# A two-layer encoder step: a new opening, biases read from one line, a gate computed in 32-column strips

## The chip, the cores and the metric

The kernel runs on one core of one Trainium2 chip. The metric is the device time of one execution, in microseconds (us), as the median of several runs. Five engines work side by side in a core: TensorE (PE in the profile, its weight loads PEld), VectorE (DVE), ScalarE (ACT), GpSimd (POOL) and SyncE (SP). Each runs its own list of instructions in order, and waits on semaphores for the others. Transfers are issued by an engine into its queue and carried by 16 DMA engines.

## The reference

One inference step of an encoder with two layers, on 256 prompt tokens and 32 sample tokens, feature width D = 1024, float32:

```
layer 0:  h = rmsnorm(x);  q,k,v of 16 heads = h @ w_in_ab
          heads 0-7:  chunked attention, softmax(q k/8 + rel_bias[clip(distance)])
          heads 8-15: stick-breaking attention
          x += concat(heads) @ w_out_ab
layer 1:  h = rmsnorm(x);  q,k,v of 16 heads and 16 forget gates = h @ w_in_c
          logf = log_sigmoid(gate + b_f);  c = cumsum(logf)
          softmax(q k/8 + c[query] - c[key]);   x += heads @ w_out_c
each layer then: x += cross_attention(rmsnorm(x), 256 memory tokens)
                 x += swiglu_ffn(rmsnorm(x))
y = rmsnorm(x);  outputs: y, all new k and v, logf, the memory's k and v
```

The sample tokens also attend to cached keys and values. The relative bias depends only on query minus key, clipped to ±128, so for each of the 8 heads one line of 384 numbers holds all that is needed.

## The kernel before, in words

**Layout.** Activations stay transposed: features on the 128 partitions, the 288 tokens along the free dimension. `x[k]`, k = 0..7, are the eight feature blocks, held in four tiles of two blocks each.

**A projection.** The weights come as "units": 128 output columns by 1024 input features, 512 KB, one tile `st` of 128x1024 (four buffers, one SP transfer). ScalarE casts a unit to `hi` (line 141) and VectorE subtracts to get `lo` (line 142); activations are split the same way into `hh` (line 247, ScalarE) and `hl` (line 250, VectorE). For every feature block `mm3` (line 145) multiplies hi by hh, hi by hl and lo by hh, so a projection (`project`, line 151) is 24 matmuls of 288 columns that add up in one PSUM bank, `pj`. Nearly all matmuls are issued in the helper `mm`, line 68.

**The norm.** The gain is multiplied in at the split, and 1/rms of each token later: squares of x (line 202, or line 200 on POOL), their sum over blocks (`ssq`, line 213), a few matmuls with a vector of 1/1024 (`nrm`), eleven small VectorE operations for the reciprocal root (lines 227 to 232), six matmuls that spread it over the partitions (`nr`), and a copy to `rstd` (line 280). Projections do not wait for that; their evacuation does: `evac_q` (line 720) and `evac_kv` (line 725) register a function with `then`, which runs when `rstd` is there and multiplies by it.

**Order of the work.** Python generators in the list `active` are advanced one step by `tick()`, which every projection calls; each `yield` is a place where a piece of attention waits for the next tick, so that a projection's matmuls cover the work of the other engines in between. A framework then orders each engine's instructions and sets the semaphores. `pairs` (line 807) projects q, k, v of two heads at a time, and adds the pair's attention to the list behind it. `memory.steps` puts projections of the memory tokens in between (`kh`, `mk`, `mkT`).

**Layer 0** (`mix_ab`, line 767): pairs 0 to 3 use chunked attention. `rel_lines` (line 735) loads the bias (`line`), extends it on VectorE (line 740), stores it to DRAM (`lined`) and writes it from there 128 times per head, eight transfers, into a DRAM tensor `skew` in which each row is one longer than the line; `rel_prompt` reads each head's tile `bi` back from it as two transfers, and POOL masks two corners. The softmax adds the bias and takes the maximum (line 350, VectorE), ScalarE takes the exponential (line 352), VectorE divides (line 355), and PE transposes the result (`tp`, lines 374 to 376).

**Layer 1** (`mix_c`, line 874): the 16 gate columns are one unit, `w_c[24]`, padded to 128 columns; it and the first q unit are begun for six of eight blocks ahead of the last blocks of x (`begin`). `gate` (line 821) scales the result by `rstd`, adds the bias (line 826), transposes it (`gt`, lines 829 to 831), takes the log-sigmoid in a chain of small VectorE and ScalarE operations (lines 834 to 847), and forms the sums over tokens by matmuls with a triangle (`gc`, `gs`, `gn`). The sums go to DRAM (`cumd`, line 858) and come back spread over the partitions (`ck`, line 896); POOL makes the bias tiles `bc` of them (lines 901 to 904), and the softmax of pair 0 needs those.

**Stores.** Keys and values (line 730), memory keys and values, and the log gates are stored by SP, in the queue that loads the weights. The result y is stored in six pieces (line 976).

Of the kernel before, what the change touches and what calls it, by code (L numbers as in the profile page):

```python
# [15 lines left out]
P = 128  # L16
NT = 288
# [9 lines left out]
def encoder_step(ctx: ExitStack, tc: tile.TileContext, a):  # L27
# [39 lines left out]
    def mm(out, lhsT, rhs, start=True, stop=True):  # L67
        T.matmul(out, lhsT, rhs, start=start, stop=stop, skip_group_check=True)  # L68
# [5 lines left out]
    first = wp.tile([P, 1024], F32, tag="st", bufs=4, name="first")  # L74

    def first_part(c0, c1):
        DMA.dma_start(first[:, c0:c1], a["w_ab"][0][:, c0:c1])

    first_part(0, 256)
    for i in range(4):  # L80
        DMA.dma_start(xh[i], a["xT"][:, 2 * i * NT:2 * (i + 1) * NT])
        if i == 0:
            DMA.dma_start(gain, a["gains"])
            first_part(256, 512)
        if i == 1:
            first_part(512, 1024)
# [5 lines left out]
    make_identity(nc, identb)  # L92

# [23 lines left out]
    for h in range(4):  # L117
        G.memset(odd[32 * h:32 * h + 32, h % 2:h % 2 + 1], 1.0)

# [7 lines left out]
    V.tensor_tensor(fold, by_head[:, :, 0], by_head[:, :, 1], ALU.add)  # L127
    wtab = cst.tile([P, 2], F32, name="wtab")
# [3 lines left out]
    def unit(src, st=None, pieces=1):  # L132

        if st is None:
            st = wp.tile([P, 1024], F32, tag="st", bufs=4, name=name("st"))
            DMA.dma_start(st, src)
        hi = wp.tile([P, 1024], F32R, tag="hi", bufs=5, name=name("hi"))
        lo = wp.tile([P, 1024], F32R, tag="lo", bufs=4, name=name("lo"))
        for c in range(pieces):
            b = slice(c * 1024 // pieces, (c + 1) * 1024 // pieces)  # L140
            S.copy(hi[:, b], st[:, b])  # L141
            V.tensor_tensor(lo[:, b], st[:, b], hi[:, b].bitcast(F32), ALU.subtract)  # L142
        return hi, lo

    def mm3(out, w, blk, h, k, start, stop):
        b = slice(blk * P, blk * P + P)
        mm(out, w[0][:, b], h[0][k], start, False)
        mm(out, w[0][:, b], h[1][k], False, False)
        mm(out, w[1][:, b], h[0][k], False, stop)

    def project(src, h, n=NT, w=None, begun=None):
        if begun:
            w, p = begun
        else:
            w, p = w or unit(src), acc("pj")
        with tc.issue_after(warmed.ins):
            for k in range(BEGIN if begun else 0, KT):
                mm3(p[:, :n], w, k, h, k, k == 0, k == KT - 1)
        tick()
        return p  # L160
# [19 lines left out]

    def start(g):
# [7 lines left out]
    class Norm:  # L189
# [7 lines left out]
        def add(self, xb, second=False, pool=False):  # L197
# [859 lines left out]
```

## Time and profile before

| | |
|---|---|
| median of 3 runs | 971.54 us (970.67 to 971.94) |
| the profiled execution | 974.15 us, its span 972.3 us |
| mean granted TensorE clock | 0.995 |
| instructions | 19122 |
| bytes moved | 163.59 MB |

The profile is of one execution, which took 974.15 us, 2.6 us over the median of the runs; its span, from the first instruction shown to the last, is 1.85 us shorter than its time. In a row of groups stand line, engine, operation, output from inputs, shape and count, then busy us and the mean ns of one, then the idle time in front and what ended it. In the chain of waits each row is one piece of the path that ended last: start, length, and the engine and line, or the transfer, that held it. A matmul's duration in the timeline is its time in the pipeline; what a matmul costs is the distance from its start to the next one's.

### The profile page before, as it was taken

To read this page: it belongs to the slowest core of one execution; us is meant where nothing else is said; L and a number is where in the kernel's file an instruction comes from. 1 tells how busy PE (TensorE), PEld (TensorE's weight loads), DVE (VectorE), ACT (ScalarE), POOL (GpSimd) and SP (SyncE) were. 2 spreads that over 40 slices of the span, in tenths; PEclk is the share of its full clock that TensorE was granted. 3 is DMA by queue.
4 is the path that set the end of the run, shared out by engine and by line. 5 is a ranking of instruction groups with operands and counts; after the bars stand their busy time and mean duration, and the time that the engine had idled before them with its cause. 6 is when DMAs were issued, how large, how long until landed. Compare 5 with 4: busy or idle time off the path is not lost.

```text
span 972.3 us, 19122 instructions
## 1 busy us (share of the span) xinstructions
PE 955.3 (98%) x7495; PEld 923.2 (95%) x7495; DVE 588.6 (61%) x1133; ACT 484.8 (50%) x856; POOL 195.1 (20%) x291
## 2 busy tenths in 40 slices
PE   8999999999999999999999999999999999999997
PEld 7889999998999999999998999999989999999996
DVE  6587555676666555754565666657757655555452
ACT  5456768545554444444444545446546544444331
POOL 3021001310213222411004333213002222222010
PEclk9999999999999999999999999999999999999999
DMA  7775455544254444554555555555434444444431
GB/s 232 247 241 189 137 180 181 183 162 147 103 174 154 173 162 164 191 192 160 173 202 161 179 190 191 169 164 179 150 117 159 159 159 173 163 164 173 165 117 49
DMA packets 59721, 163.59 MB, mean 168 GB/s; under 512 B 8192, under 2 KB 20528, under 8 KB 59632
## 3 DMA queue, kind: packets, MB, share of 16 engines
q1 hardware_dynamic: 59632, 162.38, 49.0%
q8 instruction: 59, 0.97, 0.4%
q14 instruction: 30, 0.25, 0.1%
HBM read 152.20 MB, written 11.72 MB: 169 GB/s over the span
## 4 chain that ended last, share of the span: by engine, by line
PE 91%; DMA 3%; DVE 3%; issue 1%; ACT 1%; SPq 1%; POOL 0%; DVEq 0%; POOLq 0%; ACTq 0%
PE pj L68 51%; PE dn L68 14%; PE op L68 11%; PE mv L68 5%; PE po L68 1%; PE xo L68 1%; PE xs L68 1%; DMA st<-w_ab 1%; PE zb L68 1%; PE sc L68 1%; DVE lo L142 1%; DMA skew<-lined 1%; DMA x<-xT 1%; PE xss L68 1%; PE xt L614 0%
## 5 line engine op out<-in xcount | busy, mean ns | idle before, releaser
L141 ACT CAST hi<-st 128x1024 fp32r<-128x1024 f32 x260 | 272.2, 1049 | 335.7 <-issue 147.3
L68 PE MATMUL pj<-hh,hi 128*128 128x288 f32 (+1 forms) x1352 | 406.3, 301 | 0.0
L68 PE MATMUL pj<-hl,hi 128*128 128x288 f32 (+1 forms) x1352 | 399.9, 296 | 1.7 <-DVE hl L250 1.7
L68 PE MATMUL pj<-hh,lo 128*128 128x288 f32 (+1 forms) x1352 | 400.2, 296 | 0.0
L142 DVE TENSOR_TENSOR lo<-st,hi 128x1024 fp32r<-128x1024 f32 x260 | 322.7, 1242 | 127.4 <-PE dn L68 41.2
L68 PEld LDWEIGHTS pj<-hh,hi 128*128 128x128 f32 x1352 | 257.0, 190 | 5.8 <-issue 4.2
L68 PEld LDWEIGHTS pj<-hl,hi 128*128 128x128 f32 x1352 | 257.1, 190 | 3.3 <-DVE hl L250 3.2
L68 PEld LDWEIGHTS pj<-hh,lo 128*128 128x128 f32 x1352 | 256.9, 190 | 0.0
L68 PE MATMUL dn<-fh,hi 128*128 128x288 f32 x400 | 108.5, 294 | 0.0
L68 PE MATMUL dn<-fh,lo 128*128 128x288 f32 x352 | 103.3, 294 | 0.0
L68 PE MATMUL dn<-fl,hi 128*128 128x288 f32 x304 | 89.5, 294 | 0.0
L68 PE MATMUL op<-ol,hi 128*128 128x288 f32 x256 | 75.8, 297 | 0.0
L68 PE MATMUL op<-oh,hi 128*128 128x288 f32 x256 | 75.5, 297 | 0.0
L68 PE MATMUL op<-oh,lo 128*128 128x288 f32 x256 | 75.2, 294 | 0.0
L68 PEld LDWEIGHTS dn<-fh,hi 128*128 128x128 f32 x400 | 72.3, 188 | 0.0
L68 PEld LDWEIGHTS dn<-fh,lo 128*128 128x128 f32 x352 | 66.2, 188 | 0.0
L213 POOL TENSOR_TENSOR ssq<-ssq,sq 128x288 f32<-128x288 f32 (+1 forms) x37 | 37.7, 1018 | 119.8 <-ACT sq L202 76.8
L68 PEld LDWEIGHTS dn<-fl,hi 128*128 128x128 f32 x304 | 57.1, 188 | 0.0
L695 POOL TENSOR_TENSOR fl<-us,fh 128x288 fp32r<-128x288 f32 x38 | 32.9, 865 | 119.3 <-ACT fh L694 119.3
L690 DVE TENSOR_TENSOR us<-pj,rstd 128x288 f32<-128x288 f32 x44 | 20.1, 457 | 59.9 <-PE pj L68 59.9
L691 POOL TENSOR_TENSOR gs<-gs,sg 128x288 f32<-128x288 f32 x44 | 38.9, 884 | 75.8 <-ACT sg L689 75.8
L68 PEld LDWEIGHTS op<-ol,hi 128*128 128x128 f32 x256 | 48.2, 188 | 0.6 <-issue 0.4
(257 smaller groups left out, 1204.9 us busy)
## 6 DMA issues: line engine op xcount, KB each, us to landing
st<-w_gate SPq DMA_DIRECT2D x44, 512.0 KB, 3.3
st<-w_up SPq DMA_DIRECT2D x44, 512.0 KB, 3.2
st<-w_down SPq DMA_DIRECT2D x44, 512.0 KB, 3.2
st<-w_c SPq DMA_DIRECT2D x25, 512.0 KB, 3.3
st<-w_ab SPq DMA_DIRECT2D x23, 512.0 KB, 4.4
st<-w_xk SPq DMA_DIRECT2D x16, 512.0 KB, 3.4
st<-w_xv SPq DMA_DIRECT2D x16, 512.0 KB, 3.5
st<-w_xq SPq DMA_DIRECT2D x16, 512.0 KB, 3.5
```

The lines of the kernel that those rows point to most:

```text
L68: T.matmul(out, lhsT, rhs, start=start, stop=stop, skip_group_check=True)
L141: S.copy(hi[:, b], st[:, b])
L142: V.tensor_tensor(lo[:, b], st[:, b], hi[:, b].bitcast(F32), ALU.subtract)
L213: eng.tensor_tensor(s[:, :self.n], self.acc[i][:, :self.n], q[:, :self.n], ALU.add)
L690: V.tensor_tensor(us, pu[:, :NT], cur.r, ALU.mult)
L691: G.tensor_tensor(gs, gs, sg, ALU.mult)
L695: G.tensor_tensor(lo, us, hi.bitcast(F32), ALU.subtract)
```

## The change

1. **Opening.** The first q, k and v units are loaded in three parts each, between the four tiles of x, and multiplied side by side, block by block, into three PSUM banks (`side_by_side`). All eight squares go to ScalarE and all seven sums to VectorE. The norm's first step no longer yields.
2. **Biases.** POOL loads the line at the start, extends it, and stores `lined`; the tensor `skew` is gone. Each head's tile is two transfers of 64 overlapping rows out of `lined`, and one tile serves both query tiles. The order of rows that this gives is falling, so q is written in falling order and turned back when the transposed softmax is copied.
3. **Held work.** `held` and `not_before` add orderings without a wait: the splits of the units in pairs 0 to 3 stand behind the norm's chain and an earlier projection in their engine's list, and loads of caches and memory stand behind later weights. The memory's preparation, the attention of pair 0 and that of the first sample groups start one tick later.
4. **Stores.** Keys, values, memory keys and values and log gates are stored by POOL.
5. **Gate.** The gate's weights come as 128x256, are multiplied by the gain on VectorE (`wgg`), and eight float32 matmuls of 32 columns write four strips of 32 partitions in one bank. Three float32 matmuls with `fold4` add the four strips while they transpose. The sums `gc` come one tick later, the attention of pair 0 as well; the units begun early are now the first q and k; one memory step moves from the end to pair 0.
6. **Tail.** y is stored in three pieces.

The diff, cut to its core:

```diff
-    first = wp.tile([P, 1024], F32, tag="st", bufs=4, name="first")
...
-    first_part(0, 256)
...
+    first = [wp.tile([P, 1024], F32, tag="st", bufs=4, name=f"first{i}") for i in range(3)]
+    def first_part(i, c0, c1):
+        DMA.dma_start(first[i][:, c0:c1], a["w_ab"][4 * i][:, c0:c1])
+    PARTS = ((0, 256), (256, 512), (512, 1024))
+    first_part(0, *PARTS[0])
...
             DMA.dma_start(gain, a["gains"])
-            first_part(256, 512)
-        if i == 1:
-            first_part(512, 1024)
+        if i < 3:
+            for u in range(3):
+                if i or u:
+                    first_part(u, *PARTS[i])
...
+    line = cst.tile([8, 384], F32, name="line")
+    lined = dr.tile([8, 384], F32, name="lined")
+    G.dma_start(line[:, 128:384], a["rel"][:, 0:256])
...
+    G.tensor_copy(line[:, 0:128], line[:, 128:129].to_broadcast([8, 128]))
+    G.dma_start(lined, line)
...
+    def unit_tiles():
+        return [wp.tile([P, 1024], F32R, tag=t, bufs=n, name=name(t)) for t, n in (("hi", 5), ("lo", 4))]
+    def split_weights(st, w, c0=0, c1=1024, hold=False):
+        hi, lo = (t[:, c0:c1] for t in w)
...
+    began, behind, loads = [], [], []
...
+    def not_before(ins, other):
+        tc.add_manual_dep(ins.ins, other.name, mybir.DependencyInfo(mybir.DependencyClass.NoSync, mybir.DependencyReason.DATA),
+                          reason="not_before")
+    def held(ins):
+        if hurry[0]:
+            for i in began[-2:-1] + [i for i in behind if i.engine == ins.ins.engine]:
+                not_before(ins, i)
...
+    def unit(src):
...
+        loads.append(DMA.dma_start(st, src).ins)
+        w = unit_tiles()
+        split_weights(st, w, hold=True)
+        return w
...
+    def store(dst, t):
+        G.dma_start(dst, t)
...
-        def add(self, xb, second=False, pool=False):
+        def add(self, xb, eng=None):
             q = tok("sq")
-            if pool:
-                G.tensor_tensor(q[:, :self.n], xb[:, :self.n], xb[:, :self.n], ALU.mult)
...
             self.parts += 1
...
-            else:
-                eng = V if self.parts == KT else G
-            i = int(second or (self.parts == KT and self.hurry))
+            eng = eng or (V if self.parts == KT else G)
...
-            if self.gi != 1:
+            if self.gi > 1:
...
-            S.copy(self.r, p)
-            for f in self.waiting:
-                f()
+            r = S.copy(self.r, p)
+            done = [f() for f in self.waiting]
             self.waiting = None
+            if self.gi == 0:
+                behind.append(self.norm.last.ins)
+                yield 1
+                behind.extend([r.ins, done[-1].ins])
...
+        q0, q1 = (q[:, 160:288], q[:, 32:160]) if falling else (q[:, 0:128], q[:, 128:256])
...
+                S.copy(w[hd][:, 0:384], t[:, 0:384])
...
-    def cache(src):
...
-        DMA.dma_start(t, src)
+        i = DMA.dma_start(t, src)
+        if ahead:
+            not_before(i, loads[-ahead])
...
...
                 st = wp.tile([P, 1024], F32, tag="st", bufs=4, name=name("mem"))
...
+                if self.l == 0:
+                    not_before(i, loads[-1])
...
-                DMA.dma_start(a["mkT"][l, i], t[:, 0:NP])
...
         t = tok("q")
-        cur.then(lambda: V.scalar_tensor_tensor(t, p[:, :NT], 0.125, cur.r, op0=ALU.mult, op1=ALU.mult))
+        out = t[:, ::-1] if falling else t
...
         t = tok("kv")
         def go():
-            V.tensor_tensor(t, p[:, :NT], cur.r, ALU.mult)
-            DMA.dma_start(dst, t)
+            i = V.tensor_tensor(t, p[:, :NT], cur.r, ALU.mult)
+            store(dst, t)
+            return i
...
+    def rel_prompt(h):
...
+        G.memset(t[64:128, 192:256], NEG)
+        for p, n in ((0, 256), (64, 192)):
+            G.dma_start(t[p:p + 64, 0:n], bass.AP(tensor=lined.tensor, offset=lined.offset + 384 * h + p + 1, ap=[[1, 64], [1, n]]))
...
+        G.dma_start(t[:, 0:160], bass.AP(tensor=lined.tensor, offset=lined.offset + 384 * 4 * g + 97, ap=[[384, 4], [1, NS], [1, 160]]))
...
+        def side_by_side():
+            p = [att("pj"), acc("pj"), acc("pj")]
+            with tc.issue_after(warmed.ins):
+                for k in range(KT):
+                    for u in range(3):
+                        i = mm3(p[u][:, :NT], w0[u], k, cur.h, k, k == 0, k == KT - 1)
+                        if k in (0, 5, 7) and u == 2:
+                            began.append(i.ins)
+            tick()
+            return p
...
+            hurry[0] = j < 4
             b = 12 * (j // 4) + j % 4
             kv = 8 * (j // 4) + j % 4
-            qs[j] = evac_q(cur, project(w[b], cur.h, w=w0 if j == 0 else None))
-            if j == 0:
-                proj.line = rel_lines()
-            ks[j] = evac_kv(cur, project(w[b + 4], cur.h), a["kv0"][kv])
...
+            qs[j] = evac_q(cur, next(p), j < 4)
+            ks[j] = evac_kv(cur, next(p), a["kv0"][kv])
+            if j < 4:
...
-                return attend_prompt(*args, [rel_prompt(proj.line, 2 * j + i) for i in range(2)], o[0][j], o[1][j])
...
+        def attend(j):
+            return later(attention(j), j == 0)
...
-                return attend_sample(*args, rel_sample(proj.line, g), oo)
-            return stick_sample(*args, oo)
+                bias = rel_sample(g)
+                yield 1
...
+    def later(g, n):
+        for _ in range(n):
+            yield 1
...
-        zt = tok("gz")[0:H]
...
+        V.tensor_tensor(zt, p[:, :NT], cur.r, ALU.mult)
...
-        T.transpose(t[:, 0:16], zt[:, 0:128], ident[0:H, 0:H])
-        T.transpose(t[:, 16:32], zt[:, 128:256], ident[0:H, 0:H])
-        T.transpose(t[0:NS, 32:48], zt[:, 256:288], ident[0:H, 0:H])
...
+        G.dma_start(a["lf"][0:256].rearrange("(t p) h -> p t h", p=P), lf[:, 0:32].rearrange("p (t h) -> p t h", h=H))
+        G.dma_start(a["lf"][256:288], lf[0:NS, 32:48])
+        yield 1
...
+        wg, wgg = tok("wg"), tok("wgg")
+        DMA.dma_start(wg[:, 0:256], a["w_g"])
+        g = gain[:, KT:2 * KT].unsqueeze(2).to_broadcast([P, KT, 32])
+        V.tensor_tensor(wgg[:, 0:256].rearrange("p (k c) -> p k c", c=32), wg[:, 0:256].rearrange("p (k c) -> p k c", c=32), g, ALU.mult)
         w = a["w_c"]
-        begun = begin([w[24], w[0]], cur.h)
+        begun = begin([w[0], w[8]], cur.h)
         active.append(cur.scale())
-        p = project(w[24], cur.h, begun=begun[0])
+        p = acc("gp")
+        for k in range(KT):
+            mm(p[32 * (k % 4):32 * (k % 4) + 32, :NT], wgg[:, 32 * k:32 * k + 32], x[k], k < 4, k >= 4)
...
+            qs[j] = evac_q(cur, project(w[j], cur.h, begun=begun[0] if j == 0 else None))
+            ks[j] = evac_kv(cur, project(w[8 + j], cur.h, begun=begun[1] if j == 0 else None), a["kv1"][j])
...
+            return later(attend_prompt(qs[j], ks[j], vs[j], vns, j, bias, o[0][j], o[1][j]), j == 0)
...
-        pairs(proj, attend, sample, memory, (3, 1, 1, 1, 1, 1, 1, 5))
+        pairs(proj, attend, sample, memory, (4, 1, 1, 1, 1, 1, 1, 4))
...
+    w0 = [unit_tiles() for _ in first]
...
+        if m in (1, 3, 5):
+            for st, w in zip(first, w0):
+                split_weights(st, w, *PARTS[m // 2])
     for m in range(KT):
-        cur.norm.add(x[m], m >= 4, m < 4)
+        cur.norm.add(x[m], V)
...
-            DMA.dma_start(a["y"][P * t:min(P * t + P, NT), b], out[r, b])
+        DMA.dma_start(a["y"][P * t:min(P * t + P, NT)], out[r])
```

Three places show how the order moves. On TensorE at the start of the program: `pj` is the bank, `hh` and `hl` the split x, `hi` and `lo` the split weights. Before:

```order
L68 MATMUL pj_252<-hh_166,hi_174 128x288
L68 MATMUL pj_252<-hl_167,hi_174 128x288
L68 MATMUL pj_252<-hh_166,lo_175 128x288
L68 MATMUL pj_252<-hh_170,hi_174 128x288
L68 MATMUL pj_252<-hl_171,hi_174 128x288
L68 MATMUL pj_252<-hh_170,lo_175 128x288
```

And after the change:

```order
L68 MATMUL pj_283<-hh_187,hi_181 128x288
L68 MATMUL pj_283<-hl_188,hi_181 128x288
L68 MATMUL pj_283<-hh_187,lo_182 128x288
L68 MATMUL pj_284<-hh_187,hi_183 128x288
L68 MATMUL pj_284<-hl_188,hi_183 128x288
L68 MATMUL pj_284<-hh_187,lo_184 128x288
L68 MATMUL pj_285<-hh_187,hi_185 128x288
L68 MATMUL pj_285<-hl_188,hi_185 128x288
L68 MATMUL pj_285<-hh_187,lo_186 128x288
L68 MATMUL pj_283<-hh_191,hi_181 128x288
```

Three matmuls per feature block became nine, in three banks.

On VectorE in the norm of the opening: `ssq` are the sums of squares, `lo` a unit's split, `ms` the first of the small operations. Before, four units are split ahead of it:

```order
L142 TENSOR_TENSOR lo_295<-st_292,hi_294 128x1024
L124 TENSOR_SCALAR ident<-warm 128x128
L213 TENSOR_TENSOR ssq_226<-sq_222,sq_224 128x288
L127 TENSOR_TENSOR fold<-ident 128x64
L142 TENSOR_TENSOR lo_348<-st_345,hi_347 128x1024
L213 TENSOR_TENSOR ssq_230<-ssq_226,sq_228 128x288
L142 TENSOR_TENSOR lo_401<-st_398,hi_400 128x1024
L213 TENSOR_TENSOR ssq_234<-ssq_230,sq_232 128x288
L142 TENSOR_TENSOR lo_465<-st_462,hi_464 128x1024
L227 TENSOR_SCALAR ms_330<-nrm_323 128x6
```

After, seven sums and one split:

```order
L243 TENSOR_TENSOR ssq_241<-sq_237,sq_239 128x288
L243 TENSOR_TENSOR ssq_245<-ssq_241,sq_243 128x288
L243 TENSOR_TENSOR ssq_249<-ssq_245,sq_247 128x288
L243 TENSOR_TENSOR ssq_253<-ssq_249,sq_251 128x288
L243 TENSOR_TENSOR ssq_257<-ssq_253,sq_255 128x288
L243 TENSOR_TENSOR ssq_261<-ssq_257,sq_259 128x288
L243 TENSOR_TENSOR ssq_265<-ssq_261,sq_263 128x288
L151 TENSOR_TENSOR lo_390<-st_387,hi_389 128x1024
L257 TENSOR_SCALAR ms_362<-nrm_358 128x6
```

The next units' splits now stand behind the small operations.

In SP's queue at the gate of layer 1: `cumd` and `cumsd` are the stores of the sums, `ck` the load that the bias tiles need, `mkT` a store of memory keys, `st` a unit. Before:

```order
L858 DMA cumd<-gr_6299 16x256
L865 DMA cumsd<-gw_6306 16x160
L553 DMA mkT<-mk_6316 128x256
L136 DMA st_6805<-w_c 128x1024
L553 DMA mkT<-mk_6354 128x256
L553 DMA mkT<-mk_6392 128x256
L896 DMA ck_6399<-cumd 128x512
```

After:

```order
L916 DMA cumd<-gr_6346 16x256
L923 DMA cumsd<-gw_6353 16x160
L962 DMA ck_6408<-cumd 128x512
L173 DMA st_6874<-w_xk 128x1024
L173 DMA st_6943<-w_c 128x1024
```

The load of `ck` now follows the two stores directly; the `mkT` stores are in POOL's queue.

## What will it do to the time?

> **What bounds the kernel now.** The first view is the page: the engines' busy time, and the chain of waits summed by engine.
>
> ```profile
> PE 955.3 (98%) x7495; PEld 923.2 (95%) x7495; DVE 588.6 (61%) x1133; ACT 484.8 (50%) x856; POOL 195.1 (20%) x291
> PE 91%; DMA 3%; DVE 3%; issue 1%; ACT 1%; SPq 1%; POOL 0%; DVEq 0%; POOLq 0%; ACTq 0%
> ```
>
> TensorE holds 91% of the chain, so a change gains only by fewer matmuls, or where the other 9% (some 88 us) really stops TensorE. The second view is the chain of waits over the first 40 us.
>
> ```profile
> 3.63 5.58 DMA x<-xT
> ...
> 16.27 6.79 DMA skew<-lined
> ...
> 23.14 6.50 DMA st<-w_ab
> ...
> 29.72 1.06 ACT hi L141
> ...
> 33.92 0.30 PE tp L374
> ...
> 35.67 4.06 PE pj L68 x24
> ```
>
> The last tile of x lands at 9.21. Then the writing of the skew tensor holds the queues, a weight behind it takes 6.50 us to land, and the softmax of pair 0 reaches its transposes (tp) at 33.92. The third view is a table of windows (us, then busy us and instructions of PE, PEld, DVE, ACT, POOL, the granted clock, the DMA share, GB/s), over the stages in which TensorE is slow or idle.
>
> ```profile
> 13.00:17.00 4.00, 4.00 (x19) 4.00 (x18) 3.52 (x7) 2.31 (x4) 0.00 (x0) 1.00 0.75 273
> 18.00:22.00 4.00, 4.00 (x34) 4.00 (x33) 3.23 (x12) 0.50 (x1) 0.00 (x0) 1.00 0.97 239
> 34.20:37.50 3.30, 3.28 (x15) 2.89 (x15) 1.38 (x5) 1.90 (x3) 0.00 (x0) 0.50 0.43 143
> 522.00:524.00 2.00, 0.30 (x4) 0.09 (x2) 1.21 (x9) 1.56 (x8) 0.99 (x3) 1.00 0.10 23
> 525.70:529.00 3.30, 3.30 (x16) 3.30 (x15) 0.68 (x1) 0.19 (x1) 0.00 (x0) 0.50 0.55 148
> 967.60:971.00 3.40, 0.00 (x0) 0.00 (x0) 0.54 (x1) 0.20 (x1) 0.00 (x0) 0.76 0.96 342
> ```
>
> "4.00 busy" in the first two hides a factor: 19 matmuls against 34 in the same 4 us, 0.21 and 0.118 us each. The clock column says 1.00 in both, so up to about 17 us I trust the count. At 34.2 and 525.7 the clock column itself says 0.50, each just after a stop of TensorE: the transposes at 33.92, and 522 to 524, where it worked 0.30 of 2.00 us. So three places pay here: the opening, the gate of layer 1, and perhaps the end. Between them the trace has no stop of 2 us.
>
> **The opening, step by step.** The groups of the first 40 us give the prices, the timeline the moments.
>
> ```profile
> L142 DVE TENSOR_TENSOR lo<-st,hi 128x1024 fp32r<-128x1024 f32 x6 | 7.3, 1218 | 5.4 <-ACT hi L141 5.4
> L250 DVE SCALAR_TENSOR_TENSOR hl<-x,gain,hh 128x288 fp32r<-128x288 f32 x8 | 4.9, 625 | 1.6 <-ACT hh L247 1.6
> L142 DVE TENSOR_TENSOR lo<-first,hi 128x256 fp32r<-128x256 f32 x4 | 3.2, 832 | 3.6 <-ACT hi L141 3.6
> L213 DVE TENSOR_TENSOR ssq<-ssq,sq 128x288 f32<-128x288 f32 x2 | 0.9, 446 | 0.0
> L350 DVE CUSTOM_DVE_ANT_0 e<-sc,bi 128x256 f32<-128x256 f32 x2 | 0.8, 420 | 0.0
> ```
>
> ```profile
> L247 ACT ACTIVATE hh<-x,gain 128x288 fp32r<-128x288 f32 x8 | 3.8, 527 | 2.0 <-DMA x<-xT 1.0 <-DMA gain<-gains 0.9
> L202 ACT ACTIVATE sq<-x 128x288 f32<-128x288 f32 x4 | 1.6, 435 | 0.0
> ```
>
> ```profile
> 5.13 0.61 PE L68 MATMUL pj<-hh,hi 128*128 128x288 f32 x1
> 20.25 0.17 DVE L227 TENSOR_SCALAR ms<-nrm 128x6 f32<-128x6 f32 x1 [0.49 <-PE nrm L68]
> 22.27 0.17 DVE L232 SCALAR_TENSOR_TENSOR y<-nt,y 128x6 f32<-128x6 f32 x1
> 23.33 0.75 PE L68 MATMUL nr<-ident,y 128*128 128x128 f32 x6
> 24.12 0.40 ACT L280 COPY rstd<-nr 128x288 f32<-128x288 f32 x1 [5.61 <-PE nr L68]
> 24.92 0.81 DVE L729 TENSOR_TENSOR kv<-pj,rstd 128x288 f32<-128x288 f32 x2
> 27.60 0.93 PE L68 MATMUL sc<-kv,q 64*128 64x128 f32 x8
> ```
>
> Two more units (1.05 MB) now stand ahead of the last tile of x. At 364 GB/s (273 at a share of 0.75) they take 2.9 us: it lands at 12.1 instead of 9.21. TensorE has nine matmuls per block instead of three, so it is not starved: 72 from 5.13 on, at 0.24 us each while the clock is low (twice the 0.118 of the later window). If the clock rises between 10 and 13.7, since there are no gaps any more, they end at 17 to 18.5; if only at 17, as before, at 20. I take 18.
>
> The norm runs beside this. The last two splits of x, 2 x 0.53, end at 13.2; eight squares at 0.435 end at 16.7 on ScalarE; VectorE follows with its seven sums (0.446 each) and ends the last at 17.3. A unit's lo (1.22) stands ahead of the small operations, as the order shows: 18.5. These took 22.27 + 0.17 - 20.25 = 2.2 us: 20.7. Meanwhile TensorE multiplies the fourth unit, 24 at 0.133 = 3.2 us, to 21.7; then nr, 0.75, and the copy, 0.40, so `rstd` is ready at 22.9 instead of 24.52, with one projection more behind it. The fifth unit ends at 25.65, the value transposes and scores (0.93 for the scores, 1.4 in all) at 27.05, the sixth projection, that is the seventh unit in all, at 30.25. VectorE in that time has q, two kv (0.81), q, lo, kv, lo, four maxima (0.42 for the wide ones), lo, and the divisions: the first transpose can start at about 31.0, and the six end at 32.2. Before, the same work (six transposes and the projection behind them) was done at 39.73. **Opening: -7.5 us.** The half-rate stretch after the stop goes with it, since the new stop is 0.7 us; that is in the number.
>
> Its bounds: splits as slow as the row of 832 ns for 256 columns (0.4 more in each of six) and a clock that rises late (1.5) leave 3.5; no stop at the transposes, an early clock and no lo in the way give 9.5. The bias tiles are not late by this: three transfers follow one another from the start of POOL's list (line, `lined`, tile), and even at the 5.58 of a tile of x each they are there at about 18, against a need at 27. What hides the held splits is the work of one projection, 3.2 us for 1.05 and 1.22. A later stop of the same kind, where a split stood ahead of a softmax, is this one:
>
> ```profile
> 62.05 1.14 DVE lo L142
> ```
>
> I leave it at nothing, with 1.1 us as a gain at most.
>
> [...]
>
> **The gate, step by step.**
>
> ```profile
> 173.61 25.50 PE op L68 x192
> ...
> 229.59 0.57 PE xso L68 x16
> ```
>
> ```profile
> 499.37 1.93 PE pj L68 x14
> ...
> 501.30 0.16 PE gt L829
> ...
> 508.89 0.82 PE gc L68 x4
> ...
> 510.15 0.77 PE gn L68 x6
> ...
> 516.75 3.32 issue
> ```
>
> ```profile
> 500.57 0.35 DVE L826 TENSOR_SCALAR gz<-gz,bf 16x288 f32<-16x288 f32 x1
> ```
>
> ```profile
> PE gc L68 <- DVE lf L847: 1.1, 1, 1.1
> ```
>
> - The padded unit goes: 24 matmuls at 25.50/192 = 0.133, -3.2 us. The eight new float32 ones run as 16 passes, like `xso` (0.57 for 16 passes of 128 columns, in strips of 32): scaled to 288 columns 1.3 us. Net -1.9.
> - `gt` becomes three float32 matmuls, six passes like `gn` (0.77) instead of 0.27: +0.5. Only some six matmuls now lie between `nr` and `gt` instead of 14 (1.93 us), while `gz` is ready at 500.92: +0.8 of waiting.
> - `gc` comes one tick later: of its wait of 1.1 to 1.2 us 0.4 stays: -0.8. What else enters VectorE's list there (a split, two memory evacuations) keeps it from nothing.
> - The bias tiles: `ck` stands behind `mkT` stores in SP's queue now and directly behind `cumd` after, and 24 more matmuls (3.2 us) lie ahead of the transposes of pair 0. The wait in 522 to 524 (2.00 - 0.30 = 1.7) and what the half rate after it loses (half of 3.3, 1.7) go: -3.4. Next late is the softmax itself, covered by that projection.
>
> **Gate: -4.8 us.** Bounds: with the bias wait and half rate kept 1.4 is left, and with 16 passes at the full 0.133, 0.6; call it 1.0. Without the new waits it is 6.0.
>
> **Everything else: 0.** The tail:
>
> ```profile
> 966.70 3.07 SPq L976 DMA_DIRECT2D y<-yo  x6
> ```
>
> Its window shows the DMA engines busy at 0.96, so bytes decide and three stores for six change nothing. The stores on POOL:
>
> ```profile
> L730 SPq DMA_DIRECT2D kv<-kv x32: 337/344/1256, 25.4 to 628.2; - x32
> ```
>
> On SP an issue took 0.344 us. No row shows one on POOL; the bounds are that 0.34 and, the other way, several us (rival 3). POOL is 20% busy, so 86 transfers at about 1 us would make it 29%, which hides them; taken as 0.
>
> The sum is 7.5 + 4.8 = 12.3 us less: the profiled execution from 974.15 to 961.9, and the median, 2.6 below it, from 971.54 to 959.2.
>
> **Rivals.** First: the opening is bound by ScalarE and VectorE, which split three units in parts, or by bias tiles that come late; the row of 832 ns speaks for it, the idle 3.6 us beside it against. Opening gain 3.5: 971.54 - 3.5 - 4.8 = 963.2.
>
> Second: the gate's waits move but stay, since its chain of small operations is longer than the matmuls that cover it, or the strips do not overlap. That chain goes to and fro between two engines. Gate gain 1.0: 963.0. Both together: 967.0.
>
> Third, the slow side: POOL's queue becomes the bound in pairs 0 to 3. About 20 transfers (two for each of eight bias tiles, kv stores between them) stand in its list in the 40 us from 22 to 63, and a pair's softmax waits for its bias tile behind the pair before's stores. At p us each the delay is 20p - 40 beyond the cover: nothing at 1 us, and at p = 2.6 it eats the 12.3. With 3 us: 971.54 - 12.3 + 20 = 979.2. Against it: the nearest issue row is 0.344. [...]
>
> Fourth: the orderings without waits are lost on the framework and nothing moves; the order already shows them moved, so little is left for it.
>
> **How the numbers follow.** The forecast has 0.63, the first rival 0.15, the second 0.12, the third 0.07, no change 0.03. The first three are faster: 0.90. A measurement of this kernel can tell about 0.2%, 1.9 us, from no change. The range goes from all upper bounds, 971.54 - 9.5 - 6.0 - 1.1 = 954.9, to both lower ones, 967.0, and leaves out the last two cases.
>
> **What would show it.** In the profile after: x landing near 12, `rstd` near 22.9, the first tp near 31 with a clock at 1.00 behind it; in the gate no stop of 2 us ahead of tp, and no window at 0.50 there. A late x, splits near 0.8 us for 256 columns, or TensorE idle ahead of `nr` would show the first rival. POOL's issues at over 2 us, with PE waiting for `bi` through VectorE, would show the third. Wrong altogether would be new stops in the pairs or the feed-forward parts, where I claim nothing changes.

## The result, and the profile after

The changed kernel takes 967.05 us as the median of 4 runs (965.87 to 967.96), the kernel before 971.61 of 4 beside it (970.67 to 971.94): 4.6 us less, a ratio of 0.9948 with a 95% interval of 0.9935 to 0.996. It is faster, as forecast, but by 4.6 us instead of 12.3, and 967.05 lies just outside the range of 954.9 to 967.0.

The two profiled executions are 8.3 us apart (974.15 and 965.87). That is more than the medians, because the one before lay at the upper end of its kernel's times and the one after at the lower end of its own: in the comparisons below the kernel before ran from 970.76 to 974.19. So a term that is read from this pair of profiles has to be checked against medians. First the page of the changed kernel, with busy times and the chain by engine:

```profile
PE 946.9 (98%) x7484; PEld 914.2 (95%) x7484; DVE 591.0 (61%) x1140; ACT 485.7 (50%) x862; POOL 239.9 (25%) x364
PE 91%; DVE 3%; DMA 2%; ACT 2%; issue 1%; SPq 0%; POOL 0%; DVEq 0%; ACTq 0%; POOLq 0%
```

POOL went from 195.1 to 239.9 us, TensorE is at 91% of the chain still. The chain of waits over the first 40 us (start, length, what held it):

```profile
6.97 6.67 DMA x<-xT
...
18.79 0.47 DVE ssq L243
...
19.31 0.83 PE nrm L68 x6
20.14 3.51 PE pj L68 x24
23.65 0.59 PE nr L68 x6
24.24 3.29 PE pj L68 x24
...
27.86 0.86 PE sc L68 x8
28.72 3.40 PE pj L68 x24
32.12 0.11 PE tp L409
...
33.26 3.08 PE pj L68 x23
```

From the norm's matmuls at 19.31 to 38.40 TensorE is busy throughout (19.04 of 19.09 us): the skew writes, the weight that landed 6.50 us after its issue and the stop ahead of tp are gone. Before, the work up to 33.26 here was done at 39.73. The chain of waits at the gate of layer 1:

```profile
482.08 5.66 DMA wg<-w_g
...
487.77 0.44 DVE wgg L944
...
488.25 1.18 PE gp L68 x16
...
495.11 0.84 PE nr L68 x6
...
495.97 0.41 ACT rstd L310
...
496.40 0.47 DVE gz L882
...
497.00 0.94 PE pj L68 x6
497.94 0.52 PE gt L68 x6
```

Here is what the prediction did not have: the path leaves TensorE, first for the load of the gate's weights, later for rstd and gz. The table of waits of that stretch says who waited for whom (total us, times, longest; `wg` are the gate's weights as loaded, `wgg` the same times the gain, `gp` the strips' bank):

```profile
DVE wgg L944 <- DMA wg<-w_g: 3.3, 1, 3.3
PE gp L68 <- DVE wgg L944: 1.3, 1, 1.3
PE pj L68 <- DVE gz L882: 1.1, 1, 1.1
```

And 40 us later, where the attention of pair 0 and of the first sample tokens meets its bias tiles, the stop ahead of tp is small, but a new one stands ahead of the sample's transposes (ts):

```profile
523.17 0.30 DVE e L389
...
523.60 0.30 PE tp L409
...
534.08 0.31 DVE es L389
...
534.44 0.33 PE ts L441
```

TensorE had ended the matmul ahead of ts at 533.68, so that stop is 0.8 us (the table of waits: 0.8).

How far the two profiles are apart at the same work, by the start of the same instruction in both timelines:

| | before | after | difference |
|---|---|---|---|
| layer 0, first zb (scores of pair 4) | 86.46 | 80.31 | -6.15 |
| layer 0, first op | 173.44 | 167.51 | -5.93 |
| layer 0, feed-forward, first dn | 418.30 | 412.02 | -6.28 |
| layer 1, first op | 646.72 | 638.64 | -8.08 |
| last transposes (yt) | 961.91 | 953.51 | -8.40 |

The opening gave some 6 us and layer 1 up to its first op 1.8, about the size of the half-rate stretch (1.7) that, of these two executions, only the one before had there.

### The profile page after: what moved, and what is told of

The parts are those of the page before. It is cut to its first block, busy times and chain, and to the rows that moved or that the text cites. A ratio compares the mean times of both kernels' runs of the same rounds, so it can differ in the third digit from the quotient of the medians.

```text
span 964.2 us, 19131 instructions
## 1 busy us (share of the span) xinstructions
PE 946.9 (98%) x7484; PEld 914.2 (95%) x7484; DVE 591.0 (61%) x1140; ACT 485.7 (50%) x862; POOL 239.9 (25%) x364
## 4 chain that ended last, share of the span: by engine, by line
PE 91%; DVE 3%; DMA 2%; ACT 2%; issue 1%; SPq 0%; POOL 0%; DVEq 0%; ACTq 0%; POOLq 0%
PE pj L68 51%; PE dn L68 14%; PE op L68 10%; PE mv L68 5%; PE po L68 1%; PE xo L68 1%; DMA x<-xT 1%; PE zb L68 1%; PE sc L68 1%; PE xs L68 1%; DMA st<-w_ab 1%; DMA wg<-w_g 1%; PE nrm L68 1%; PE xss L68 1%; ACT hi L150 1%
## 5 line engine op out<-in xcount | busy, mean ns | idle before, releaser
L150 ACT CAST hi<-st 128x1024 fp32r<-128x1024 f32 x257 | 269.1, 1050 | 321.9 <-issue 142.8
L68 PE MATMUL pj<-hh,hi 128*128 128x288 f32 (+1 forms) x1344 | 400.9, 298 | 1.1 <-DVE gz L882 1.1
L68 PE MATMUL pj<-hl,hi 128*128 128x288 f32 (+1 forms) x1344 | 395.6, 294 | 0.0
L68 PE MATMUL pj<-hh,lo 128*128 128x288 f32 (+1 forms) x1344 | 394.7, 294 | 0.4 <-DVE lo L151 0.4
L68 PEld LDWEIGHTS pj<-hh,hi 128*128 128x128 f32 x1344 | 253.2, 188 | 7.1 <-issue 5.4
L68 PEld LDWEIGHTS pj<-hh,lo 128*128 128x128 f32 x1344 | 253.3, 188 | 1.1 <-DVE lo L151 1.0
L68 PEld LDWEIGHTS pj<-hl,hi 128*128 128x128 f32 x1344 | 253.3, 188 | 0.5 <-issue 0.5
```

Of the source, the lines that this page charges most:

```text
L68: return T.matmul(out, lhsT, rhs, start=start, stop=stop, skip_group_check=True)
L150: a = S.copy(hi, st[:, c0:c1])
```

## The experiments

**The theory** that these readings suggest: the opening did what was forecast; the gate's strips took away 24 matmuls that were the cover of the norm and of the gate's chain, and put new waits in their place; and the stop ahead of tp in layer 1 went for a reason of its own. **The rival:** the strips are worth their 3 us, and POOL's queue or the new opening takes them back elsewhere. The kernel before, run beside each group of experiments, took 972.41 us in experiments 1 to 4, 972.49 in 5 to 8 and 972.34 in 9 to 12 (medians of 17 or 18 runs); each ratio is to that.

### 1. The gate's weights early

```diff
+        if layer == 0:
+            wg = tok("wg")
+            DMA.dma_start(wg[:, 0:256], a["w_g"])
...
-        DMA.dma_start(wg[:, 0:256], a["w_g"])
```

> The changed kernel with one thing moved: the 128 KB of gate weights are loaded at the start of the feed-forward part of layer 0 instead of at the start of layer 1. Theory: the changed kernel's VectorE waits 3.3 us for these weights and TensorE stops 1.5 us ahead of the strips; with the load early that stop goes and the time falls by 1.5 us, from 967.05 to about 965.5, with the first strip following a matmul at 0.13 to 0.2 us. Rival: the stop is only moved to the next link of the gate (the wait for gz or the chain before gc grows by as much), and the time stays within 0.5 us of 967.

Measured: 966.07 us (965.19 to 966.14), ratio 0.9933 [0.9922, 0.9945], against 0.9948 for the changed kernel. That is 1.0 us less in time, 1.5 by the ratios; the intervals overlap. In its profile the stop ahead of the strips is gone. But the stop at gz stays, and in this execution it was followed by half the clock. The windows around it (us, busy us and counts of PE, PEld, DVE, ACT, POOL, clock, DMA share, GB/s):

```profile
494.40:496.40 2.00, 0.95 (x9) 0.98 (x9) 1.77 (x5) 0.40 (x1) 0.00 (x0) 1.00 0.47 164
497.40:500.60 3.20, 3.20 (x17) 3.20 (x17) 0.18 (x1) 1.70 (x4) 0.54 (x1) 0.50 0.26 101
```

The same stop and the stretch behind it in the changed kernel's profile:

```profile
495.70:497.00 1.30, 0.23 (x3) 0.15 (x3) 1.16 (x3) 0.63 (x2) 0.00 (x0) 1.00 0.31 123
497.40:500.60 3.20, 3.20 (x29) 3.15 (x28) 1.09 (x5) 1.77 (x3) 1.12 (x2) 1.00 0.54 207
```

17 matmuls against 29 in 3.2 us, behind a stop of about the same length. The 12 missing ones are 1.6 us at 0.133: such a stop costs 1.1 us in one execution and some 2.7 in another.

### 2. The strips' bank from the other group as well

```diff
-        p = acc("gp")
+        p = att("gp")
```

> As the run before it, and the strips' bank is taken from the other group of four banks, so that the next projection doesn't wait until gz has read it. Theory: the 1.2 us stop between nr and the next projection goes as well: about 964.3. Rival: gt waits for gz in its place, since gz is not ready earlier, and the time is that of the run before, about 965.5, or the other group's banks run short and a score or transpose waits, 966 to 967.

Measured: 965.99 us (964.74 to 966.47), 0.9931 [0.9919, 0.9943]. No difference in time from the run before it, though the stop ahead of the projection is gone from the profile. The rival holds in kind: the wait moved to the next link, the sums `gc` at the end of the gate's chain. TensorE's wait ahead of them in experiment 1, then in this run:

```profile
PE gc L68 <- DVE lf L904: 0.4, 1, 0.4
```

```profile
PE gc L68 <- DVE lf L904: 1.5, 1, 1.5
```

The 1.1 us that gz no longer takes stand there in full. The stop ahead of ts is still there (0.7).

### 3. The new opening with the old gate

```diff
-        begun = begin([w[0], w[8]], cur.h)
+        begun = begin([w[24], w[0]], cur.h)
...
+        p = project(w[24], cur.h, begun=begun[0])
...
-        pairs(proj, attend, sample, memory, (4, 1, 1, 1, 1, 1, 1, 4))
+        pairs(proj, attend, sample, memory, (3, 1, 1, 1, 1, 1, 1, 5))
```

with `gate` as before.

> The changed kernel with the gate of before (padded unit, transposes, steps and ticks as before); opening, biases, held splits, stores and tail as changed. Theory: nearly all of the measured gain is the opening's, 971.6 less 4 to 5, that is 966.6 to 967.6, and the gate's new waits took what its fewer matmuls gave. Rival: the gate has its gain of several us and the opening gives little: 969 to 970.

Measured: 964.71 us (964.64 to 965.82), 0.9924 [0.9912, 0.9936]: 7.7 us under before, and below the changed kernel. The theory had expected 966.6 to 967.6; the gain is larger, so the gate's edit as a whole (strips, later ticks, the moved memory step) does not merely give nothing, it costs some 2.3 us. The two were timed in different groups, and their intervals just touch (0.9936 and 0.9935). And the old gate has no stop ahead of the transposes of pair 0 (515.93 here) either; in the 1.80 us before them TensorE is busy throughout:

```profile
514.10:515.90 1.80, 1.80 (x15) 1.62 (x14) 1.16 (x7) 1.80 (x8) 0.82 (x3) 1.00 0.86 285
```

So that stop goes without the strips and without the later tick as well.

### 4. The kernel before with the new gate alone

The complement of experiment 3: before, with `gate`, `mix_c`, `fold4` and the packing of the weights as changed, stores on SP.

> The kernel before with the new gate alone (strips, ticks, memory steps; stores on SP as before). Theory: 0 to 2 us under before, 969.6 to 971.6, with TensorE stopping for the gate's weights and for gz. Rival: the gate alone gives the forecast 4.8, 966.8, and it is the stores on POOL or the opening that take it back in the changed kernel.

Measured: 972.46 us (970.5 to 974.89, 12 runs), 1.0001 [0.9992, 1.001]: nothing. That is the end of the theory at which nothing is gained; the rival's 4.8 us is not there even without POOL's stores. Its trace shows what the later tick does by itself: POOL still waits 2.8 us for `ck`, but TensorE's stop ahead of the transposes of pair 0 is down to 0.3 us, and a stop of 1.4 us stands ahead of ts instead. The half-rate stretch of the profile before is not in it (clock 1.00 from 525.00 to 529.00).

### 5. The new opening, the old gate, and the stores back on SP

```diff
     def store(dst, t):
-        G.dma_start(dst, t)
+        DMA.dma_start(dst, t)
```

> The run with the new opening and the old gate (964.71), with all stores of keys, values, memory keys and values and log gates back in SP's queue. Theory: what freed the gate of layer 1 was not the strips but that the load of ck no longer stands behind three mkT stores in SP's queue; so TensorE's stop of some 1.7 us ahead of the transposes of pair 0 in layer 1 comes back, with a half-rate stretch in part of the executions: 966.4 to 968. Rival: the stores' queue is without effect, and the old gate's stop went because the work around it shifted: 964.2 to 965.2.

Measured: 967.17 us (965.9 to 968.12), 0.9947 [0.9935, 0.9959]: 2.5 us more than with the stores on POOL. The stop is back:

```profile
516.10:517.60 1.50, 0.24 (x2) 0.01 (x1) 1.12 (x7) 1.06 (x6) 0.55 (x3) 1.00 0.08 9
```

and the table of waits around it shows the chain behind it, POOL's tile on the load, VectorE on POOL, TensorE on VectorE:

```profile
POOL bc L958 <- DMA ck<-cumd: 3.0, 1, 3.0
DVE e L384 <- POOL bc L961: 2.4, 2, 1.6
...
PE tp L409 <- DVE e L389: 1.5, 2, 1.3
```

The theory holds: the load of `ck` stood behind the three mkT stores in SP's list. SP issues it 5.3 us behind `cumd` here (504.26 to 509.53), and 3.3 us behind it in experiment 3 (503.87 to 507.16).

### 6. The kernel before with its stores on POOL

```diff
-            DMA.dma_start(dst, t)
+            G.dma_start(dst, t)
```

and likewise for mkT, mv and the log gates.

> The kernel before with its stores issued by POOL, nothing else. Theory: the same 1.7 to 3.4 us less as the run beside it gives back, 969 to 970.7 against 972.4, with an issue on POOL at 0.55 us. Rival: POOL's list holds up its tensor work and nothing is gained, 972 to 973.

Measured: 969.46 us (968.37 to 971.33), 0.9969 [0.9957, 0.998]: 3.0 us less from this edit alone. The price of an issue on POOL, in the groups of this run:

```profile
L730 POOL DMA_DIRECT2D kv<-kv x32 | 17.9, 560 | 82.6 <-DVE kv L729 76.7 <-DVE hh L249 5.7
```

0.56 us against 0.344 on SP: the issue is dearer, and the run is 3.0 us shorter all the same. POOL has the time (20% busy before, 25% after the change), and SP's list has loads that others wait for (POOL 3.0 us for `ck` in experiment 5).

### 7. The first three units one after the other

```diff
-                for k in range(KT):
-                    for u in range(3):
+                for u in range(3):
+                    for k in range(KT):
```

in the kernel of experiment 3.

> The run with the new opening and the old gate (964.71), with the first three units multiplied one after the other, each over all eight blocks, in place of side by side; loads, splits, norm and biases as they are. Theory: the gain of the opening comes from nine matmuls per block that are ready as x lands; one by one, TensorE can do only the first unit's three per block until the last x at 13.6, and 48 matmuls are left then, 6.3 us or more at the full rate against some 30 side by side: 2.5 to 5 us more, 967 to 970. Rival: the norm chain bounds the opening and the 48 matmuls fit beside it until rstd: under 1 us more, 965 to 965.7.

Measured: 967.69 us (967.62 to 969.72), 0.9956 [0.9943, 0.9968]: 3.0 us more than side by side. In its chain 53 matmuls were left when the split of x that they waited for was there, at 14.61, and the norm's matmuls stand behind them, 4.1 us later than after the change:

```profile
14.61 8.80 PE pj L68 x53
23.41 0.56 PE nrm L68 x6
```

The work that was left is not all of it. The clock was also at half from 12.00 to 18.00, behind a stop of TensorE (0.46 busy of 2.20 us from 9.00 on); 53 matmuls at 0.133 would be 7.0 us, not 8.80. In this run, then in the changed kernel:

```profile
12.00:18.00 6.00, 5.81 (x21) 4.92 (x22) 5.32 (x14) 5.74 (x13) 2.49 (x7) 0.50 0.94 289
```

```profile
9.00:13.00 4.00, 4.00 (x29) 3.65 (x27) 2.98 (x8) 2.61 (x6) 2.43 (x5) 1.00 1.02 383
```

So side by side gives two things, which this run does not separate: less work left, and a TensorE that is at the full clock from 9.00 to 13.00 (1.00 in that window).

### 8. The splits not held

```diff
     def held(ins):
-        if hurry[0]:
+        if False:
```

in the kernel of experiment 3.

> The run with the new opening and the old gate (964.71), with the splits of pairs 0 to 3 not held behind the norm (the order of ScalarE's and VectorE's lists is then the framework's own). Theory: three further splits of 1.22 us stand among VectorE's small operations ahead of rstd, rstd comes 3 to 4 us later, but TensorE has projections to do meanwhile; the softmax of pair 0 is later by that and waits: 1.5 to 3.5 us more, 966.2 to 968.2. Rival: the projections cover it, within 0.5 us of 964.7.

Measured: 971.75 us (970.2 to 973.85, 11 runs), 0.9993 [0.9984, 1.0002]: 7.0 us more: more than the 5.3 that the opening gives with the stores on SP (experiment 5), and twice the upper end of what the theory expected. The chain shows a weight's landing and its cast on ScalarE ahead of the last squares, and `rstd` 11 us later than after the change:

```profile
12.25 7.75 DMA st<-w_ab
20.03 1.04 ACT hi L150
...
22.75 0.94 ACT hi L150
23.70 0.47 DVE ssq L243
...
35.38 0.41 ACT rstd L310
```

and the windows a stop of TensorE from 18.5 to 24.2, with the clock at half behind it:

```profile
18.50:24.20 5.70, 0.15 (x2) 0.00 (x0) 2.33 (x6) 4.17 (x8) 0.00 (x0) 0.75 0.89 314
25.90:31.60 5.70, 5.70 (x25) 5.70 (x25) 2.71 (x6) 0.89 (x2) 0.00 (x0) 0.50 0.81 264
```

The theory's mechanism was wrong in one point: TensorE has no projection to do meanwhile. The fourth unit's split had ended at 18.07, but in TensorE's list the norm's matmuls stand ahead of that projection, and they wait for the sums:

```profile
24.21 1.44 PE L68 MATMUL nrm<-mean,ssq 128*128 128x2 f32 x6 [5.57 <-DVE ssq L243]
```


### 9. The skew's traffic put back, unread

```diff
+    skew = dr.tile([8, 128 * 385], F32, name="skew")
+    for h in range(8):
+        DMA.dma_start(bass.AP(tensor=skew.tensor, offset=skew.offset + h * 128 * 385, ap=[[385, P], [1, 384]]),
+                      bass.AP(tensor=lined.tensor, offset=lined.offset + 384 * h, ap=[[0, P], [1, 384]]))
```

> The run with the new opening and the old gate (964.71), with the eight writes of the skew tensor (192 KB each) put back into SP's queue behind the line's store; nothing reads them. Theory: they hold up the third unit and those behind it by about the 6 us that they took before, so a projection in the first 50 us waits for its weights or the softmax of pair 0 stops as it did: 2 to 5 us more, 966.7 to 969.7. Rival: the weights are loaded far enough ahead, three units being there from the start, and it costs under 0.7 us: 964.5 to 965.4.

Measured: 967.76 us (967.0 to 969.66), 0.996 [0.9948, 0.9972]: 3.0 us more, within the theory's range. How it costs that is not settled. In the profiled execution the transposes of pair 0 come 1.4 us later than in experiment 3, and that is one stretch at half rate behind the short stop ahead of nrm, not a late weight (the mean clock of this execution is 0.995, against 0.998 in experiment 3):

```profile
21.60:24.70 3.10, 3.10 (x15) 3.10 (x14) 2.06 (x6) 0.00 (x0) 0.00 (x0) 0.50 1.05 210
```

### 10. The strips with their three new waits removed

Experiment 2, with the first sample attention of layer 1 one tick later:

```diff
-            return attend_sample([qs[j] for j in two], ...
+            return later(attend_sample([qs[j] for j in two], ..., g == 0)
```

> The strips with their weights early and their bank in the other group (965.99), with the attention of the first two pairs' sample tokens in layer 1 one tick later, so that its transposes don't wait for POOL's bias tile. Theory: the stop of 0.9 us ahead of these transposes goes: about 965.1, no better than the old gate with the same opening (964.7), since the matmuls that the strips save are those which covered the norm and the gate's chain. Rival: the strips are a gain once their waits are gone: under 963.5.

Measured: 964.46 us (962.69 to 966.77), 0.9927 [0.9914, 0.994]: 1.5 us less than experiment 2 by the medians, 0.4 by the ratios, and the same as the old gate (0.9924). The stop ahead of ts is gone, the wait ahead of gc stays at 1.5 us (1.1 with the old gate). Its best execution is 2.0 us under the best of the old gate, its median equal: so the strips can be brought to the old gate's level, not clearly below it. Those two best executions are the profiled ones, and their traces place the 2.0: 0.96 stand already at the first zb (79.15 against 80.11), where the two kernels are the same; 0.84 arise between the first dn of layer 0 and the first op of layer 1 (224.43 against 225.27 us). That is what is left of some 2 us of matmuls saved (3.2 less 1.18), and it shows in no median.

### 11. Some squares and sums on POOL

```diff
-        cur.norm.add(x[m], V)
+        cur.norm.add(x[m], G if m < 3 else V)
```

with squares and sums on POOL for G, in the kernel of experiment 3.

> The run with the new opening and the old gate (964.71), with the first three squares and two of the sums of the first norm on POOL instead of ScalarE and VectorE. Theory: TensorE's stop of 1.2 us at nrm is the length of the squares and sums after the last x; three squares (1.3 us) and three sums (1.4 us) fewer there end it: 0.8 to 1.2 us less, 963.5 to 963.9. Rival: POOL's slower operations (about 1 us each) come late behind its first transfers, or slow VectorE beside them, and the time is the same or up to 1 us more.

Measured: 966.13 us (964.66 to 967.2), 0.9936 [0.9925, 0.9948]: 1.4 us more by the median; the theory fell, the rival holds (0.4 over its bound). Beside POOL's operations VectorE's splits of 512 columns took 1151 ns, against 692 in the changed kernel, so the sums end no earlier (19.31, against 19.26). The profiled execution (964.66) is as fast as that of experiment 3, so no trace shows where the others lose the 1.4. In this run, then in the changed kernel:

```profile
L151 DVE TENSOR_TENSOR lo<-first,hi 128x512 fp32r<-128x512 f32 x3 | 3.3, 1151 | 0.0
```

```profile
L151 DVE TENSOR_TENSOR lo<-first,hi 128x512 fp32r<-128x512 f32 x3 | 2.1, 692 | 0.7 <-ACT hi L150 0.7
```

### 12. The kernel before with its splits held

```diff
+            i = S.copy(hi[:, b], st[:, b])
...
+            if pieces == 1:
+                held(i)
+                held(j)
```

> The kernel before with the splits of pairs 0 to 3 held as in the change, nothing else. Theory: holding matters only once three units are multiplied at the start and TensorE has nothing left to do until the norm is done; in the kernel before TensorE has projections to do until the biases come, so it gives at most 1 us: 971.4 to 972.6 against 972.4. Rival: the held order is the gain by itself: 968 or less.

Measured: 973.02 us (971.31 to 973.8, 11 runs), 1.0004 [0.9995, 1.0012]: nothing, as expected (0.4 us above the range given). Holding the splits is worth 7.0 us beside the three units and nothing without them.

## Why the prediction was wrong, by its own steps

**The opening, -7.5: right in mechanism, too large.** By medians it gave 5.3 us (experiment 5 against before: 972.49 to 967.17), by the two profiles 6. The clock rose earlier than at 10 to 13.7, the author's estimate: the trace's clock record stands at full from 8.54 on, before only from 17.06 on; no run shows what sets that moment. What came later were transfers and sums, 1.1 to 2.0 us at each step. The last x landed at 13.64, not 12.1: the sum had only the bytes of the two units, but SP issues six more parts ahead of that tile, some 0.46 us each, so it went out at 6.97 (before: 4.1). The last sum ended at 19.26, not 17.3: the squares were done at 17.31, but VectorE began its seven sums at 15.42, behind its own splits, and took some 0.55 us for each with the gaps between them (the working had 0.446). `rstd` was ready at 24.7, not 22.9; the first tp came at 32.1, not 31.0, and its six were done at 33.26, not 32.2. That the 72 matmuls ended at 18.24, close to the 18 that was taken, is luck: the late x and the early clock made up for each other.

The 7.5 also contained a half-rate stretch (1.7) which belonged to the one profiled execution: the profile of experiment 4, with the old opening as well, has none behind the transposes (clock 1.00 from 33.50 to 37.00). That a stop of 0.7 us would bring none was the author's estimate; in the changed kernel's profile the clock record stands at full from 8.54 to 960.85. There TensorE also stops for 0.7 us at a later pair's transposes (0.64 busy of 1.30 from 69.90 on). The held splits, which the working treated as hidden work, are the part on which all the rest hangs (experiments 8 and 12).

**The gate, -4.8: wrong, and here the prediction failed.** The step that failed is its first bullet, "Net -1.9", read as a gain of time. The 24 matmuls were the cover of a chain that does not get shorter: norm, rstd, gz, gt, log-sigmoid, gc. With them gone the waits came out elsewhere: for the weights (1.3 us, a load that the sum did not have at all, in SP's queue behind a unit and the loads of the caches), for gz (1.1, forecast at 0.8), for the sample's bias tile (0.8, not forecast: one tick later for the chain, but not for that consumer). Experiment 2 shows the chain directly: take gz's wait away, and gc waits 1.1 us longer. Without the wait at the bias tiles, which has its own paragraph, this edit was to give 1.4 us; it cost some 2.3 beside the new opening (0.9948 against 0.9924) and gave nothing alone (1.0001). The strips themselves were priced right, 1.18 us of path against 1.3, and so nearly was gc (0.6 us of wait, forecast 0.4).

The traces add up to about half of that. From 484 to 546 TensorE's waits come to 4.3 us in the changed kernel and to 1.3 in experiment 3, so 3.0 more; some 2.0 of matmuls went, and gt costs 0.25 more (0.52 against 0.27): 1.25 us more. Measured, from the first dn of layer 0 to the first op of layer 1, are 1.35 us more (226.62 against 225.27). Why the medians are a further 1.0 apart no trace shows; a half-rate stretch behind the new stops in some of the executions, as in experiment 1 (1.6 us), would do it, but that is an estimate.

**The wait at the bias tiles, -3.4: the stop went, and the queue alone is enough for it.** The bullet named two reasons, the queue and 24 more matmuls ahead. Experiments 3, 5 and 6 show that moving the stores ends the stop, with the old gate; it is worth 2.5 to 3.0 us by medians, near the 3.4, though that is the price of the whole move of the stores and not of this stop alone. The second reason works too, but only shifts the stop to the sample's transposes (experiment 4: 0.3 us ahead of tp, 1.4 ahead of ts). So the 3.4 was put to the gate, but would have come with no new gate at all.

**POOL's stores at 0:** their price was inside the bounds (0.55 us, where the working took about 1 as an estimate; sum 48 us of POOL's time, 25% busy), and hidden. Rival three did not come.

**The rivals.** The second, "waits move but stay", is what happened, at more than its price, except that the wait at the bias tiles went. The first had a gain of 3.5 for the opening, and its reason did not come: splits of 256 columns took 427 ns after the change, not 832. Both together gave 967.0, and that the time fell there is luck: the opening gave more than 3.5, the gate less than nothing. The forecast gave the two 0.27 as single cases and nothing as a pair.

The steps from before over experiments 5 and 3 to the changed kernel are -5.3 for the opening, -2.5 for the stores and +2.3 for the gate, together -5.4 before rounding, against forecasts of -7.5, -3.4 and -1.4. They add up by construction (972.49 to 967.05), so their sum is no test of them; beside its own runs of before (971.61) the change gave 4.6, or 5.1 by the ratio.

## What to carry to other kernels

Matmuls that cover a chain of small operations are not simply saved by deleting them: before counting a removed matmul as time, follow the chain that ran beneath it and see whether it ends before its new consumer. A queue's order is worth a look ahead of any arithmetic: moving stores out of the list that issues urgent loads gave 3 us by itself, although each issue became dearer (0.56 us against 0.344). And one profile is one execution: a stop of about 1.1 us had a stretch at half rate behind it in experiment 1 (clock 0.50) and none in the changed kernel (1.00), so a gain from ending one should be counted at less than its full length.

## What the hardware showed that was not expected

A stop of TensorE of about 1.1 us was followed by 3.2 us at half the clock in one execution (experiment 1) and by the full clock in another (the changed kernel). In the kernel before with held splits a stop of 1.7 us (0.22 of 1.90 busy) was followed by it, in the same place as in the profile of before:

```profile
521.50:523.40 1.90, 0.22 (x2) 0.00 (x0) 1.11 (x8) 1.45 (x8) 0.97 (x3) 1.00 0.21 61
525.50:528.60 3.10, 3.10 (x15) 3.10 (x14) 0.36 (x1) 0.00 (x0) 0.00 (x0) 0.50 0.58 181
```

while the stop of 1.26 us (0.24 of 1.50 busy) in experiment 5 was not: its profile has no such stretch (mean clock 0.999).

In the profile of before the clock record changes at 17.06, 34.12, 37.54, 525.64 and 529.06, so the half-rate stretches from 34.12 and from 525.64 last 3.41 us each. The same length ahead of the half rate in before and in experiment 1, and around the stop of experiment 5:

```profile
522.23:525.64 3.41, 1.55 (x11) 1.19 (x11) 2.78 (x12) 2.97 (x9) 0.76 (x3) 1.00 0.03 7
```

```profile
493.90:497.31 3.41, 2.34 (x21) 2.20 (x20) 2.63 (x8) 0.95 (x3) 0.59 (x1) 1.00 0.63 234
```

```profile
514.90:518.31 3.41, 2.06 (x14) 1.55 (x13) 2.46 (x14) 2.52 (x9) 1.75 (x6) 1.00 0.36 129
```

TensorE was busy for 1.55 and 2.34 us in the first two, and for 2.06 in the third, behind which the clock stayed full. So neither the length of the stop nor the busy time around it decides it alone in these runs, and what does is open.

The strips of 32 columns on four groups of partitions overlapped here: 16 passes of 288 columns took 1.18 us of the path, where a full matmul of 288 columns costs 0.133, and 16 of those 2.1.
